# A one-core encoder layer: the stretch before the first products is rewritten, and phase 1 gets more load buffers

## The chip, the core and the metric

The kernel runs on one core of one Trainium2 chip. The metric is the device time of one execution in microseconds. Of three runs of the kernel before, the median is 971.41 us (969.67 to 974.25).

## The reference

The program computes one layer of an encoder over 512 rows of 2048 numbers (x), all in float32. What matters for the change is its front:

```
c_act = silu(c)                                   # c: 2048 numbers
mod   = c_act @ w_ada + b_ada                     # w_ada: 2048 x 6144
shift, scale, gate = split(mod, 3)
h     = rms_norm(x, norm_gain) * (1 + scale) + shift
proj  = h @ w_in                                  # w_in: 2048 x 7168
...                                               # attention on 8 heads, retention on 4 heads
x     = x + gate * (y @ w_out)                    # w_out: 2048 x 2048
return rms_norm(x, final_gain)
```

rms_norm divides each row by the root of the mean of its squares (plus 1e-6) and multiplies the columns by a gain.

## The kernel before

**Tiling.** The 512 rows are four row tiles t of 128; the 2048 columns are sixteen tiles k of 128. h is kept transposed, one tile of 128 x 512 for each k, split into a high part hh and a low part hl; each tile of w_in is split in the same way into whi and wlo by `conv` (ScalarE copies the high part, line 543, VectorE subtracts it, line 544). A product is three passes over TensorE (`mm3`, lines 85 and 87): high by high, high by low, low by high.

**The prelude** (lines 89 to 455) makes h of column tile k = 0 and x transposed (xT) for the other fifteen. Its loads all go through SyncE's queue, in this order: c, eight loads of w_ada (256 KB each: the columns of shift and of scale that belong to k = 0), the rows of b_ada and of the gain, then x in eight halves of 512 KB. ScalarE turns c into silu(c) (`ct`). VectorE multiplies the w_ada rows by `ct` and adds them up in `acc0` (lines 279 and 281), and four narrow products with a column of ones close the sum (`sums0`, line 288). For each row tile ScalarE takes the squares (line 302), VectorE and GpSimd make the root (lines 308, 315, 319), VectorE puts the factors on a diagonal (`dg`, line 327), TensorE turns x (line 343 by a transposition, line 351 by a product with the diagonal, which also scales), and the turned tile is scaled while it is read from PSUM (line 373). `pin` makes each engine keep to the written order of the pinned instructions.

**Phase 1** (lines 873 to 974) is thirteen units of 256 columns of w_in, taken through the sixteen k in chunks of 1, 2, 2, 3, 4 and 4 tiles. During one chunk the pieces that make the next chunk's modulation are spread between the fed items (`ada_pieces`): loads of w_ada into three buffers (AR = 3, lines 202 and 205), their weighted sums on VectorE (line 216), the closing sums (lines 230 and 244), then hh on ScalarE (line 168) and hl on VectorE (line 181). `feed` loads an item, splits it four items later (LEAD = 4) and multiplies it two items after that (LOOK = 2). The raw tiles of w_in have three buffers (RAW = 3). Sums of eleven units over the chunks are kept in SBUF and added to by VectorE (line 941; in the first chunk ScalarE copies them, line 939).

**Order.** Loads of w_in and w_ada share SyncE's queue, which works through its rows one after the other: a load whose buffer or whose semaphore is not free holds back all loads behind it. The program has eight semaphores for loads, given out in turn over both hardware queues (DMAHW0 to DMAHW7 in the rows below), so a load waits until the one that had the same semaphore has landed.

## Time and profile before

| | |
|---|---|
| span of the profiled execution, which is also its time in the profile | 971.6 us |
| TensorE busy in it | 941.5 us |
| VectorE busy in it | 618.0 us |
| first product of phase 1 begins | 28.75 us after the span's start |
| chunk 0 of phase 1 ends, first product of chunk 1 | 49.2 us, 53.18 us |

Positions are microseconds from the start of the span. The page's second part cuts the span into 40 slices of 24.3 us; the stretch that the change touches is slices 1 to 9. Where a row of a window gives busy time, a stretch minus the busy time is idle time, and PEclk below 1.00 is a TensorE clock below full speed.

### The profile page before, as it was taken

What the parts mean: (1) busy time and instruction counts of PE and PEld (TensorE: products, weight loads), DVE (VectorE), ACT (ScalarE), POOL (GpSimd) and SP (SyncE); (2) the same over time, 40 slices, a digit from 0 to 9 for tenths busy, and PEclk for the clock granted to TensorE, in tenths of its full rate; (3) what the DMA queues carried; (4) which work ended last, traced back from release to release, by engine and by line L of the source; (5) the groups of instructions that cost most, each with busy time, mean ns of one, the idle gap of its engine ahead of it and who ended that gap; (6) DMA issues with size and microseconds to landing.
All of it is one profiled execution on the core that took longest, in us unless ns stands there. A gap on an engine that the chain in (4) does not pass through costs nothing.

```text
span 971.6 us, 14377 instructions
## 1 busy us (share of the span) xinstructions
PE 941.5 (97%) x5556; PEld 820.4 (84%) x5556; DVE 618.0 (64%) x1101; ACT 376.5 (39%) x732; POOL 10.6 (1%) x22
## 2 busy tenths in 40 slices
PE   5989898999999999999999999999999999999996
PEld 4877687788988888988998899988899988888896
DVE  5879978977968786664555556745534382535444
ACT  3824242525235555444343232422333372333321
POOL 0000000000000000000000000000000000000001
PEclk9989999999999999999999999999999999999999
DMA  9786878763552222212224525425322148233304
GB/s 316 232 260 209 270 250 290 266 202 99 183 179 84 65 66 66 65 45 88 84 69 161 186 66 184 143 88 198 126 63 90 57 159 283 86 128 134 109 1 173
DMA packets 109715, 141.49 MB, mean 146 GB/s; under 512 B 6024, under 2 KB 78408, under 8 KB 109648
## 3 DMA queue, kind: packets, MB, share of 16 engines
q1 hardware_dynamic: 108496, 138.49, 43.4%
q10 hardware_dynamic: 1152, 2.10, 0.6%
q8 instruction: 43, 0.70, 0.3%
q14 instruction: 24, 0.20, 0.1%
HBM read 136.36 MB, written 4.20 MB: 145 GB/s over the span
## 4 chain that ended last, share of the span: by engine, by line
PE 89%; DMA 5%; DVE 3%; issue 2%; SPq 1%; ACT 0%; POOLq 0%; POOL 0%; DVEq 0%; ACTq 0%
PE pp L87 26%; PE pw L87 14%; PE pp L85 13%; PE po L87 12%; PE pw L85 7%; PE po L85 6%; PE op L87 3%; PE sp L87 2%; DMA raw<-in_w_in_dram 2%; DMA araw<-in_w_ada_dram 2%; PE op L85 2%; PE tp L770 1%; DVE aacc L216 1%; PE sp L85 1%; DMA xt<-in_x_dram 1%
## 5 line engine op out<-in xcount | busy, mean ns | idle before, releaser
L543 ACT CAST whi<-raw 128x512 fp32r<-128x512 f32 (+1 forms) x289 | 174.9, 606 | 435.8 <-PE pp L87 204.9
L544 DVE TENSOR_TENSOR wlo<-raw,whi 128x512 fp32r<-128x512 f32 (+1 forms) x289 | 193.9, 672 | 209.6 <-ACT whi L543 205.3
L85 PE MATMUL pp<-whi,hh 128*128 128x256 f32 x576 | 162.4, 282 | 0.0
L87 PE MATMUL pp<-wlo,hh 128*128 128x256 f32 x576 | 161.9, 281 | 0.0
L87 PE MATMUL pp<-whi,hl 128*128 128x256 f32 x576 | 161.5, 280 | 0.0
L85 PEld LDWEIGHTS pp<-whi,hh 128*128 128x128 f32 x576 | 108.5, 188 | 2.5 <-ACT sc L839 1.7
L87 PEld LDWEIGHTS pp<-wlo,hh 128*128 128x128 f32 x576 | 108.5, 188 | 1.0 <-DVE wlo L544 0.2
L87 PEld LDWEIGHTS pp<-whi,hl 128*128 128x128 f32 x576 | 108.5, 188 | 0.0
L85 PE MATMUL pw<-hh,whi 128*128 128x512 f32 x256 | 102.5, 401 | 3.6 <-DVE acc L941 3.6
L85 PE MATMUL pp<-hh,whi 128*128 128x512 f32 x256 | 102.7, 403 | 3.3 <-ACT hh L168 2.9
L87 PE MATMUL pp<-hh,wlo 128*128 128x512 f32 x256 | 102.1, 399 | 0.0
L87 PE MATMUL pp<-hl,whi 128*128 128x512 f32 x256 | 101.6, 397 | 0.0
L87 PE MATMUL pw<-hh,wlo 128*128 128x512 f32 x256 | 101.3, 396 | 0.0
L87 PE MATMUL pw<-hl,whi 128*128 128x512 f32 x256 | 101.1, 395 | 0.1
L87 PE MATMUL po<-wlo,yh 128*128 128x512 f32 (+1 forms) x252 | 92.6, 367 | 0.0
L85 PE MATMUL po<-whi,yh 128*128 128x512 f32 (+1 forms) x252 | 92.5, 367 | 0.0
L87 PE MATMUL po<-whi,yl 128*128 128x512 f32 (+1 forms) x252 | 92.5, 367 | 0.0
L216 DVE SCALAR_TENSOR_TENSOR aacc<-araw,ct,aacc 128x512 f32<-128x512 f32 (+2 forms) x75 | 76.1, 1014 | 10.8 <-DMA araw<-in_w_ada_dram 10.3
L941 DVE TENSOR_TENSOR acc<-acc,pw 128x512 f32<-128x512 f32 x100 | 66.3, 682 | 7.8 <-PE pw L87 7.3
L991 DVE SCALAR_TENSOR_TENSOR gacc<-graw,ct,gacc 128x512 f32<-128x512 f32 x60 | 45.0, 750 | 38.3 <-DMA graw<-in_w_ada_dram 38.0
L85 PEld LDWEIGHTS pp<-hh,whi 128*128 128x128 f32 x256 | 48.8, 191 | 16.7 <-ACT hh L168 3.0
L85 PEld LDWEIGHTS pw<-hh,whi 128*128 128x128 f32 x256 | 48.1, 188 | 17.3 <-DVE acc L941 5.7
(232 smaller groups left out, 1555.3 us busy)
## 6 DMA issues: line engine op xcount, KB each, us to landing
raw<-in_w_in_dram SPq DMA_DIRECT2D x94, 512.0 KB, 3.5
araw<-in_w_ada_dram SPq DMA_DIRECT2D x32, 512.0 KB, 5.5
graw<-in_w_ada_dram SPq DMA_DIRECT2D x64, 256.0 KB, 2.9
raw<-in_w_out_dram SPq DMA_DIRECT2D x32, 512.0 KB, 3.5
araw<-in_w_ada_dram SPq DMA_DIRECT2D x40, 256.0 KB, 3.7
raw<-in_w_in_dram SPq DMA_DIRECT2D x16, 384.0 KB, 5.4
araw<-in_w_ada_dram SPq DMA_DIRECT2D x16, 384.0 KB, 3.7
xt<-in_x_dram SPq DMA_DIRECT2D x8, 512.0 KB, 8.6
```

The source lines that it names most:

```text
L85: nc.tensor.matmul(o, lh, rh, start=start, stop=False, skip_group_check=True)
L87: nc.tensor.matmul(o, a, b, start=False, stop=stop and b is (rl if swap else rh), skip_group_check=True)
L216: ins = nc.vector.scalar_tensor_tensor(acc[:, :, :n], rv[:, a], ct[:, kr + a : kr + a + 1], acc[:, :, :n], op0=ALU.mult, op1=ALU.add,)
L543: c1 = nc.scalar.copy(dh, src)
L544: c2 = nc.vector.tensor_tensor(dl, src, f32(dh), op=ALU.subtract)
L770: nc.tensor.transpose(tp_[:, j * P : (j + 1) * P], pt[:, j * P : (j + 1) * P], ident)
L941: nc.vector.tensor_tensor(accs[u][i], accs[u][i], ps[i], op=ALU.add)
L991: nc.vector.scalar_tensor_tensor(st["acc"], raw, ct[:, kr : kr + 1], st["acc"], op0=ALU.mult, op1=ALU.add)
```

## The change

- **Loads of the prelude.** x goes through ScalarE's queue in four loads of 1 MB; w_ada's first columns go through SyncE's in four loads of 512 KB, behind c; the rows of b_ada and of the gain go through GpSimd's queue.
- **x is scaled first, then turned.** Once a row tile's factor is known, VectorE multiplies x itself by it (`scaled`, in three pieces of 128, 896 and 1024 columns), TensorE only transposes, and the result is copied out of PSUM by ScalarE (three banks) and VectorE (one bank). The diagonal, its spreading over the partitions and the products with it are gone. The squares of a tile are split: ScalarE takes 1024 columns, VectorE the other 1024; ScalarE takes those of the next tile before it copies out this one.
- **w_ada's first columns** are no longer summed by VectorE. TensorE multiplies them by `ct` directly: 32 products of a 128 x 128 tile with one column, sixteen ahead of the last row tile's first transposition and sixteen behind it.
- **Phase 1.** w_ada has six buffers (AR = 6) in place of three, and w_in in the first four chunks three more (`raw1`). In these chunks an item is split eight items after it is fed (LEAD1 = 8) in place of four. All loads of chunk 0 are issued ahead of its first item.

ScalarE, from the start of its program. `ce` is the first step of silu(c), `xt` a row tile of x, `sq` and `sqa` the squares. Before:

```order
L144 ACT_TABLE_LOAD
L144 ACTIVATE ce<-ps_145 128x16 [waits PE_49]
L302 ACTIVATE sq,ssx<-xt_122 128x1024 [waits DMAHW3_49]
L302 ACTIVATE sq,ssx<-xt_122 128x1024 [waits DMAHW4_49,Activation_49]
L302 ACTIVATE sq,ssx<-xt_125 128x1024 [waits DMAHW5_49,Activation_49]
```

After:

```order
L121 DMA xt_107<-in_x_dram 128x2048
L121 DMA xt_108<-in_x_dram 128x2048
L121 DMA xt_109<-in_x_dram 128x2048
L121 DMA xt_110<-in_x_dram 128x2048 [waits DMAHW3_49]
L145 ACT_TABLE_LOAD
L145 ACTIVATE ce<-ps_135 128x16 [waits PE_49]
L300 ACTIVATE sqa,ssx<-xt_107 128x1024 [waits DMAHW0_49]
```

Four loads now stand ahead of the table load and of `ce`, and the fourth waits for the semaphore DMAHW3, which it shares with an earlier load.

TensorE, the end of the prelude and the first products (`pw`). `raw_105` and `raw_106` are the first columns of w_ada, for shift and for scale; `xt_109` and `xt_110` are the last two row tiles. After:

```order
L328 MATMUL psx<-ident,xt_109 128x128 x7
L286 MATMUL psa<-ct,raw_105 128x1 [waits DMAHW2_49]
L286 MATMUL psa<-ct,raw_105 128x1 x7
L286 MATMUL psa<-ct,raw_106 128x1 [waits DMAHW3_49]
L286 MATMUL psa<-ct,raw_106 128x1 x7
L322 MATMUL psk_285<-ident,xt_110 128x128 [waits DMAHW3_49,DVE_49,PE_49]
L286 MATMUL psa<-ct,raw_105 128x1 [waits DMAHW5_49]
L286 MATMUL psa<-ct,raw_105 128x1 x7
L286 MATMUL psa<-ct,raw_106 128x1 [waits DMAHW6_49]
L286 MATMUL psa<-ct,raw_106 128x1 x7
L328 MATMUL psx<-ident,xt_110 128x128 [waits DVE_49,PE_49,Activation_49]
```

The first load of `raw_106` is the one whose semaphore the fourth load of x waits for. Before, the place of these products was four, early in the prelude:

```order
L343 MATMUL psx<-ident,xt_122 128x128 x3
L288 MATMUL psa<-ones,acc_160 128x1 [waits DVE_49]
L288 MATMUL psa<-ones,acc_160 128x1
L288 MATMUL psa<-ones,acc_161 128x1 [waits DVE_49]
L288 MATMUL psa<-ones,acc_161 128x1
L331 MATMUL psb<-dg,ones 128x128 [waits DVE_49]
```

VectorE, one row tile of the prelude after the change (`sqd` is the squares' waste, `ms` the mean, `rsx` the factor that GpSimd makes, `xT` x transposed):

```order
L305 ISA sqd,ssx<-xt_108 128x1024 [waits DMAHW4_49]
L305 ISA ssx 128x1
L308 SCALAR_TENSOR_TENSOR ms_202<-ssx 128x1 [waits DVE_49,Activation_49]
L336 COPY xT_93<-psx 128x2x128 [waits PE_49]
L336 COPY xT_94<-psx 128x128
L276 COPY bg<-ps_135 128x48 [waits PE_49]
L277 TENSOR_SCALAR bg<-bg 128x16 [waits DVE_49]
L316 TENSOR_SCALAR xt_108<-xt_108,rsx 128x128 [waits Pool_49]
L316 TENSOR_SCALAR xt_108<-xt_108,rsx 128x896
L316 TENSOR_SCALAR xt_108<-xt_108,rsx 128x1024
```

All of a tile's squares, its copies and its scaling stand in one row; the next tile's squares come behind them.

The diff, cut to its core:

```diff
@@ -37,15 +37,13 @@
 N_PERSIST = 2
 ADA_SPAN = 0.65
 TAB_SPAN = 16
-WARM = 9
-WARM2 = 1
-LATE_AT = 7, 8
+WARM = 10, 3, 3
 LAG = 3
-RAW, WB, LOOK, LEAD, EB, YB = 3, 3, 2, 4, 1, 22
+RAW, RAW1, WB, LOOK, LEAD, LEAD1, EB, YB = 3, 3, 3, 2, 4, 8, 1, 22
 GR = 2
 GATE_RATE = 0.9
 N_FIRST = 13
-AR = 3
+AR = 6
@@ -73,7 +71,13 @@
     def f32(ap):
         return ap.bitcast(F32)
+    early = {"on": True, "n": 0}
     def raw_tile():
+        early["n"] += 1
+        if early["on"] and early["n"] % 2 == 0:
+            return aap.tile([P, 1024], F32, tag="raw1", name="raw1", bufs=RAW1)
         return wp.tile([P, 1024], F32, tag="raw", name="raw", bufs=RAW)
...
+    raw0 = [xp.tile([P, NK, P], F32, name=f"raw0{b}") for b in range(2)]
+    xn = [xp.tile([P, D], F32, name=f"xt{t}") for t in range(NT)]
+    def load0(q, b, i):
+        q.dma_start(
+            raw0[b][:, i * 8 : (i + 1) * 8],
+            wa[i * 8 * P : (i + 1) * 8 * P, b * D : b * D + P].rearrange("(a p) f -> p a f", p=P),
+        )
+    for t in range(NT):
+        nc.scalar.dma_start(xn[t], x2[t * P : (t + 1) * P, :])
+    nc.sync.dma_start(c_row, c.rearrange("b (k p) -> (b k) p", p=P))
+    for i in range(2):
         for b in range(2):
-            nc.sync.dma_start(
-                rv[:, :, b],
-                wa[n * 4 * P : (n + 1) * 4 * P, b * D : b * D + P].rearrange("(a p) f -> p a f", p=P),
-            )
-            if n + b == 0:
-                nc.sync.dma_start(c_row, c.rearrange("b (k p) -> (b k) p", p=P))
-        raw0.append(rv)
-        if n == 1:
-            nc.sync.dma_start(bg_row[0:32, :], b_ada[:, 0 : 2 * D].rearrange("b (k p) -> (b k) p", p=P))
-            nc.sync.dma_start(bg_row[32:48, :], norm_gain.rearrange("b (k p) -> (b k) p", p=P))
+            load0(nc.sync, b, i)
+    nc.gpsimd.dma_start(bg_row[0:32, :], b_ada[:, 0 : 2 * D].rearrange("b (k p) -> (b k) p", p=P))
+    nc.gpsimd.dma_start(bg_row[32:48, :], norm_gain.rearrange("b (k p) -> (b k) p", p=P))
...
-    acc0 = [aap.tile([P, 2 * P], F32, tag="acc0", name="acc0") for _ in range(2)]
-    for k in range(NK):
-        rv, c1 = raw0[k // 4][:, k % 4], ct[:, k : k + 1]
-        if k < 2:
-            nc.vector.tensor_scalar_mul(acc0[k], rv, c1)
-        else:
-            nc.vector.scalar_tensor_tensor(acc0[k % 2], rv, c1, acc0[k % 2], op0=ALU.mult, op1=ALU.add)
-    rsb = aap.tile([P, S], F32, name="rsb", bufs=1)
...
+    def turn_rows():
+        pin(nc.tensor.transpose(ps0[:, 64:112], bg_row, ident[0:48, 0:48]))
+        pin(nc.vector.tensor_copy(bg, ps0[:, 64:112]))
+        pin(nc.vector.tensor_scalar_add(bg[:, 16:32], bg[:, 16:32], 1.0))
+    psa = bank(psA, "psa")
+    psk = bank(psA, "psk")
+    def sums0(b, i):
+        for a in range(8 * i, 8 * i + 8):
+            pin(
                 nc.tensor.matmul(
+                    psa[:, b : b + 1], raw0[b][:, a, :], ct[:, a : a + 1],
+                    start=a + b == 0, stop=a == NK - 1, skip_group_check=True,
                 )
+            )
+    def shift_scale0():
+        pin(nc.vector.tensor_tensor(sv[:, 0:1], psa[:, 0:1], bg[:, 0:1], op=ALU.add))
+        pin(nc.vector.tensor_tensor(av[:, 0:1], psa[:, 1:2], bg[:, NK : NK + 1], op=ALU.add))
+        pin(nc.vector.tensor_tensor(av[:, 0:1], av[:, 0:1], bg[:, 32:33], op=ALU.mult))
+    def squares_a(t):
+        sa = aap.tile([P, 1024], F32, tag="araw", name="sqa", bufs=AR)
+        marks["sq"] = pin(nc.scalar.activation(sa, xn[t][:, 0:1024], AF.Square, accum_out=ssx[:, t, 0:1]))
+    def squares(t):
+        sd = aap.tile([P, 1024], F32, tag="aacc", name="sqd")
+        v = xn[t][:, 1024:2048]
+        pin(nc.vector.tensor_tensor_reduce(sd, v, v, 1.0 / D, EPS, ALU.mult, ALU.add, ssx[:, t, 1:2]))
+        ms = small.tile([P, 1], F32, tag="ms1", name="ms1", bufs=2)
         pin(
             nc.vector.scalar_tensor_tensor(
+                ms, ssx[:, t, 0:1], 1.0 / D, ssx[:, t, 1:2], op0=ALU.mult, op1=ALU.add
             )
         )
+        nc.gpsimd.tensor_tensor(rsx[:, t : t + 1], ms, mhalf[:, 0:1], op=ALU.pow)
+    def scaled(t, a, b):
+        v = xn[t][:, a:b]
+        marks["sc"] = pin(nc.vector.tensor_scalar_mul(v, v, rsx[:, t : t + 1]))
     psx = {}
+    def k0_part(t):
+        o = psk3[:, 0:P] if t == 3 else psk[:, t * P : (t + 1) * P]
+        pin(nc.tensor.transpose(o, xn[t][:, 0:P], ident))
+    def turned(t, b, pin=pin):
         ps = psx[t, b] = bank(psP, "psx")
         for j in range(b == 0, 4):
             k = 4 * b + j
             pin(nc.tensor.transpose(ps[:, j * P : (j + 1) * P], xn[t][:, k * P : (k + 1) * P], ident))
+    def evacuated(t, b, eng):
         for i, g in enumerate(groups):
             lo, hi = max(g[0], 4 * b), min(g[-1] + 1, 4 * b + 4)
             if i and lo < hi:
+                dst = xt_tiles[i][:, lo - g[0] : hi - g[0], t * P : (t + 1) * P]
+                src = psx[t, b][:, (lo - 4 * b) * P : (hi - 4 * b) * P].rearrange("p (k f) -> p k f", k=hi - lo)
+                pin(eng(dst, src))
+    act, dve = nc.scalar.copy, nc.vector.tensor_copy
...
-    for _ in range(WARM):
-        pin(nc.tensor.matmul(ps0[:, 128:256], ones, ident, start=True, stop=True))
-    turned(0, 0)
-    turned(0, 1)
-    for _ in range(WARM2):
-        pin(nc.tensor.matmul(ps0[:, 128:256], ones, ident, start=True, stop=True))
-    turned(0, 3)
-    for t in range(2):
-        squares(t, 0)
-        squares(t, 1)
-    roots(0)
-    psa = sums0()
-    psk = bank(psA, "psk")
-    diagonal(0)
-    shift_scale0(psa)
-    spread(0)
-    k0_part(0)
-    spread_out(0)
-    for t in range(2):
-        turned_scaled(t, 2)
-        evacuated(t, 2)
-        squares(t + 2, 0)
-        squares(t + 2, 1)
-        scaled(t, 0)
-        turned(t + 1, 0)
-        half_root(t + 1)
...
+    def warm(n):
+        for _ in range(n):
+            pin(nc.tensor.matmul(ps0[:, 128:256], ones, ident, start=True, stop=True))
+    warm(WARM[0])
+    squares_a(0)
+    for t in range(NT):
+        squares(t)
+        if t:
+            evacuated(t - 1, 0, dve)
         if t == 1:
+            turn_rows()
+        if t == 3:
+            psk3 = bank(psM, "psk3")
+            sums0(0, 0)
+            sums0(1, 0)
+        scaled(t, 0, P)
+        k0_part(t)
+        if t == 3:
+            break
+        scaled(t, P, 1024)
+        turned(t, 0)
+        turned(t, 1)
+        scaled(t, 1024, D)
+        turned(t, 2)
+        turned(t, 3)
+        if t < 2:
+            warm(WARM[1 + t])
+        squares_a(t + 1)
+        for b in range(1, 4):
+            evacuated(t, b, act)
+    sums0(0, 1)
+    marks["conv1"] = [marks["sq"], marks["sc"]]
+    sums0(1, 1)
+    scaled(3, P, 1024)
+    shift_scale0()
     A, B = slice(0, 3 * P), slice(3 * P, S)
     h0_sum(A, psk[:, A])
     h0_sum(B, psk3[:, 0:P])
     h0_low(A)
     h0_low(B)
+    scaled(3, 1024, D)
+    for b in range(4):
+        turned(3, b, lambda ins: ins)
+    late = [lambda b=b: evacuated(3, b, act if b % 2 else dve) for b in range(4)]
...
             if item["load"]:
                 item["load"]()
             loaded.append(item)
-        if len(loaded) > (LEAD if item is not None else 0):
+        lead = LEAD1 if early["on"] else LEAD
+        while len(loaded) > (lead if item is not None else 0):
             it = loaded.pop(0)
             pending.append((it, it["conv"]()))
-        if len(pending) > (LOOK if item is not None else 0):
+            if item is None:
+                break
+        while len(pending) > (LOOK if item is not None else 0):
             flush_one()
+            if item is None:
+                break
...
-    for i, f in zip(LATE_AT, late):
-        agenda.setdefault(i, []).append(f)
+    for i, f in enumerate(late):
+        agenda.setdefault(LEAD1 + LOOK + i, []).append(f)
...
+        early["on"] = ci < len(CHUNKS) - 2
...
+        if ci == 0:
+            for it in items:
+                it["load"]()
```

More of the change, by code (lines that the diff above doesn't have):

```diff
@@ L282, in trunk_kernel @@
-    rsb = aap.tile([P, S], F32, name="rsb", bufs=1)
-    def sums0():
-        psa = bank(psA, "psa")
-        for i in range(2):
-            for b in range(2):
+    def turn_rows():
[7 more added lines that the diff above has]
+            pin(
@@ L288, in sums0 @@
                 nc.tensor.matmul(
-                    psa[:, b : b + 1], acc0[i][:, b * P : (b + 1) * P], ones[:, 0:1],
-                    start=i + b == 0, stop=i == 1, skip_group_check=True,
-                )
-        return psa
-    def shift_scale0(psa):
-        nc.vector.tensor_tensor(sv[:, 0:1], psa[:, 0:1], bg[:, 0:1], op=ALU.add)
-        nc.vector.tensor_tensor(av[:, 0:1], psa[:, 1:2], bg[:, NK : NK + 1], op=ALU.add)
-        nc.vector.tensor_tensor(av[:, 0:1], av[:, 0:1], bg[:, 32:33], op=ALU.mult)
@@ L299, in squares @@
-    def squares(t, h):
-        sq = xp.tile([P, 1024], F32, tag="sq", name="sq")
-        v = xn[t][:, h * 1024 : (h + 1) * 1024]
-        marks["sq"] = pin(nc.scalar.activation(sq, v, AF.Square, accum_out=ssx[:, t, h : h + 1]))
-    mss = {}
-    def half_root(t):
-        ms = mss[t] = small.tile([P, 2], F32, tag="ms2", name="ms2", bufs=2)
-        pin(nc.vector.tensor_scalar(ms[:, 0:1], ssx[:, t, 0:1], 1.0 / D, EPS, op0=ALU.mult, op1=ALU.add))
-    def roots(t):
-        if t not in mss:
-            half_root(t)
-        ms = mss[t]
+                    psa[:, b : b + 1], raw0[b][:, a, :], ct[:, a : a + 1],
@@ L314, in roots @@
+    def squares(t):
[3 more added lines that the diff above has]
+        ms = small.tile([P, 1], F32, tag="ms1", name="ms1", bufs=2)
         pin(
             nc.vector.scalar_tensor_tensor(
-                ms[:, 1:2], ssx[:, t, 1:2], 1.0 / D, ms[:, 0:1], op0=ALU.mult, op1=ALU.add
+                ms, ssx[:, t, 0:1], 1.0 / D, ssx[:, t, 1:2], op0=ALU.mult, op1=ALU.add
@@ L317, in roots @@
             )
         )
-        nc.gpsimd.tensor_tensor(rsx[:, t : t + 1], ms[:, 1:2], mhalf[:, 0:1], op=ALU.pow)
-    dgs = {}
-    psbs = {}
-    def diagonal(t):
-        dg = dgs[t] = xp.tile([P, P], F32, tag="dg", name="dg", bufs=2)
-        marks["dg"] = pin(nc.vector.tensor_scalar_mul(dg, ident, rsx[:, t : t + 1]))
-    def spread(t):
-        psb = bank(psA, "psb")[:, 0:P]
-        pin(nc.tensor.matmul(psb, ones, dgs[t], start=True, stop=True))
-        psbs[t] = psb
-    def spread_out(t):
-        pin(nc.vector.tensor_copy(rsb[:, t * P : (t + 1) * P], psbs[t]))
+        nc.gpsimd.tensor_tensor(rsx[:, t : t + 1], ms, mhalf[:, 0:1], op=ALU.pow)
@@ L343, in turned @@
             pin(nc.tensor.transpose(ps[:, j * P : (j + 1) * P], xn[t][:, k * P : (k + 1) * P], ident))
-    def turned_scaled(t, b):
-        ps = psx[t, b] = bank(psP, "psx")
-        for j in range(4):
-            k = 4 * b + j
-            pin(
-                nc.tensor.matmul(
-                    ps[:, j * P : (j + 1) * P], xn[t][:, k * P : (k + 1) * P], dgs[t], start=True, stop=True
-                )
-            )
-    def pieces(b):
+    def evacuated(t, b, eng):
         for i, g in enumerate(groups):
@@ L429, in trunk_kernel @@
-    marks["conv1"] = [marks["sq"]]
-    psk3 = bank(psM, "psk3")
-    turned_scaled(2, 2)
-    turned_scaled(2, 3)
-    roots(3)
-    scaled(2, 0)
-    turned(3, 0)
-    diagonal(3)
-    marks["conv1"].append(marks["dg"])
-    k0_part(3)
+    def warm(n):
[7 more added lines that the diff above has]
+            evacuated(t - 1, 0, dve)
+        if t == 1:
+            turn_rows()
[18 more added lines that the diff above has]
+            evacuated(t, b, act)
@@ L439, in trunk_kernel @@
+    sums0(0, 1)
[3 more added lines that the diff above has]
+    shift_scale0()
     A, B = slice(0, 3 * P), slice(3 * P, S)
-    evacuated(2, 2)
     h0_sum(A, psk[:, A])
-    scaled(2, 1)
-    turned(3, 1)
     h0_sum(B, psk3[:, 0:P])
@@ L446, in trunk_kernel @@
     h0_low(B)
-    spread(3)
-    turned(3, 2)
-    evacuated(2, 3)
-    turned(3, 3)
-    spread_out(3)
-    scaled(3, 0)
-    scaled(3, 1)
-    late = [lambda b=b: scaled(3, b) for b in (2, 3)]
+    scaled(3, 1024, D)
+    for b in range(4):
+        turned(3, b, lambda ins: ins)
+    late = [lambda b=b: evacuated(3, b, act if b % 2 else dve) for b in range(4)]
     x_scope.close()
```

41 lines of the change are left out of this document (removed).

## The prediction

> **What bounds the kernel now.** I read the page first.
>
> ```profile
> span 971.6 us, 14377 instructions
> PE 941.5 (97%) x5556; PEld 820.4 (84%) x5556; DVE 618.0 (64%) x1101; ACT 376.5 (39%) x732; POOL 10.6 (1%) x22
> PE   5989898999999999999999999999999999999996
> DVE  5879978977968786664555556745534382535444
> ```
>
> TensorE is busy for 941.5 of 971.6 us, so the change can win only what TensorE loses outside its work: about 30 us, and what it does at a lower clock. The second row of digits shows VectorE near its limit in the slices up to 200 us. Then I asked for windows, to see where TensorE's losses lie (columns: the stretch, its length, busy time of PE, PEld, DVE, ACT, POOL with counts, PEclk, share of the DMA engines, GB/s).
>
> ```profile
> 48.00:50.00 2.00, 1.60 (x12) 1.12 (x10) 1.73 (x3) 0.37 (x1) 0.00 (x0) 1.00 0.88 288
> 50.00:52.00 2.00, 0.23 (x3) 0.15 (x2) 0.39 (x3) 0.20 (x1) 0.00 (x0) 1.00 1.09 368
> 52.00:54.00 2.00, 0.82 (x2) 0.73 (x3) 1.56 (x3) 2.00 (x4) 0.00 (x0) 0.54 1.06 328
> 54.00:56.00 2.00, 2.00 (x8) 1.71 (x8) 1.90 (x4) 0.45 (x1) 0.00 (x0) 0.50 0.69 255
> 56.00:58.00 2.00, 2.00 (x6) 1.55 (x6) 1.62 (x3) 0.00 (x0) 0.00 (x0) 0.50 0.39 102
> 58.00:60.00 2.00, 2.00 (x8) 1.57 (x7) 0.00 (x0) 0.33 (x1) 0.00 (x0) 0.75 0.86 245
> 110.00:116.00 6.00, 4.60 (x20) 3.09 (x18) 5.83 (x9) 1.13 (x2) 0.00 (x0) 1.00 0.80 267
> 116.00:122.00 6.00, 4.46 (x31) 3.99 (x31) 4.46 (x7) 3.01 (x13) 0.00 (x0) 1.00 0.83 284
> 140.00:170.00 30.00, 26.27 (x162) 22.48 (x162) 25.46 (x35) 7.11 (x13) 0.00 (x0) 1.00 0.83 284
> ```
>
> TensorE idles 0.40 + 1.77 + 1.18 = 3.35 us at the border from chunk 0 to chunk 1, then works at a reduced clock (0.82 x 0.46 + 2 x 0.5 + 2 x 0.5 + 2 x 0.25 = 2.9 us lost); it idles 1.40 + 1.54 = 2.94 us at 110 to 122, and 30.00 - 26.27 = 3.73 us at 140 to 170. Together **12.9 us**. The rest lies ahead of the first product and at the kernel's end. The chain of waits says what ended these stalls:
>
> ```profile
> 44.91 6.79 DMA raw<-in_w_in_dram
> 51.80 0.62 ACT whi L543
> 52.41 0.72 ACT hh L168
> ...
> 113.54 5.24 DMA araw<-in_w_ada_dram
> ...
> 144.99 5.78 DMA araw<-in_w_ada_dram
> ```
>
> At 51.8 the high part of a w_in tile waited for a load issued at 44.9, and hh of chunk 1 stood behind it on ScalarE. The later ones are VectorE's sums, waiting for w_ada with three buffers.
>
> **The change part by part. (a) What the loads now wait for.** ScalarE's fourth load of x waits until the first load of `raw_106` has landed, and behind it stand the table load, silu(c), and so all of VectorE's prelude. I call the time of that landing R. Rows for the rates:
>
> ```profile
> 2.00:13.00 11.00, 4.17 (x20) 3.77 (x20) 5.84 (x19) 0.20 (x2) 0.00 (x0) 1.00 0.99 286
> 13.00:21.50 8.50, 6.58 (x40) 5.91 (x41) 4.75 (x19) 6.01 (x10) 1.11 (x2) 0.80 1.03 413
> 0.73 1.28 ACT L144 ACT_TABLE_LOAD   x1 [0.73 <-PEq L1296]
> 5.56 0.35 DVE L279 TENSOR_SCALAR acc<-araw,ct 128x256 f32<-128x256 f32 x1 [0.35 <-DMA araw<-in_w_ada_dram]
> ```
>
> The first stretch is w_ada alone (286 GB/s), the second x alone (413 GB/s). Two loads of w_ada (1.05 MB) cost 3.7 us, each load of x (1.05 MB) 2.5 us. Data flows from about 2.3 us, and I estimate 1.3 us from last byte to release, from VectorE's first sum: it waited until 5.56 for the first two loads, whose 0.53 MB at 286 GB/s from 2.3 us were through at 4.2. If both queues get equal bytes, R = 2.3 + 3.7 + 2.5 + 1.3 = 9.8. If the three loads of x go wholly first, R = 2.3 + 7.6 + 3.7 + 1.3 = 14.9. No row shows two queues with unequal rows at once. I take **R = 10.5**, nearer the even end since both queues start together, and keep both ends.
>
> **(b) From R to the first product.** The fourth load's issue 0.5, the table load 1.28, then silu to `ct` 0.9 (ScalarE 0.18 and three small VectorE steps): R + 2.7. Then VectorE's chain per row tile:
>
> ```profile
> L755 DVE CUSTOM_DVE_ANT_0 pt<-sp,ad 128x512 f32<-128x512 f32 x32 | 21.0, 685 | 0.5 <-PE sp L87 0.5
> L762 DVE TENSOR_SCALAR pt<-pt,den 128x512 f32<-128x512 f32 x32 | 15.5, 484 | 0.6
> L802 DVE TENSOR_SCALAR dt<-dlt,lg 128x896 f32<-128x896 f32 x4 | 2.7, 682 | 0.0
> L327 DVE TENSOR_SCALAR dg<-ident,rsx 128x128 f32<-128x128 f32 x4 | 1.1, 287 | 0.7 <-POOL rsx L319 0.4
> 16.61 0.56 POOL L319 TENSOR_TENSOR rsx<-ms,mhalf 128x1 f32<-128x1 f32 x1 [15.11 <-DVE ms L315]
> ```
>
> Squares of 1024 columns: 0.685 for 512, so about 1.3 with the read of the sum; the mean 0.16; the root 0.75 from mean to next VectorE step (16.45 to 17.20 before), filled by the copies of the last tile; scaling 0.29 + 0.68 + 0.75 (128, 896, 1024 columns, the last drawn out from 0.484 and 0.682). Sum 3.9, with gaps 4.0. Three tiles: 12.0, so R + 14.7. TensorE's last eight transpositions of tile 2: 1.0. Then the 32 narrow products. Before, four took 0.95 us:
>
> ```profile
> L281 DVE SCALAR_TENSOR_TENSOR acc<-araw,ct,acc 128x256 f32<-128x256 f32 x14 | 5.7, 478 | 0.0
> 15.56 0.95 PE L288 MATMUL psa<-ones,acc 128*128 128x1 f32 x8
> 18.14 1.92 PE L351 MATMUL psx<-dg,xt 128*128 128x128 f32 x8
> 22.43 1.06 PE L351 MATMUL psx<-dg,xt 128*128 128x128 f32 x8
> ```
>
> So 32 take **7.6 us**, where VectorE's sums (14 x 0.478 = 5.7 us, hidden under x's landing) and 0.95 us on TensorE stood. They are off VectorE, but pinned on TensorE behind tile 2, and nothing covers them: VectorE needs only 2.5 us for tile 3 up to its factor. 3.8 + 0.3 (tile 3's first transposition) + 3.8. Then shift and scale 0.45, with a low part of w_in (0.69) written between, and hh's first part 0.68: 1.8. First product: R + 14.7 + 1.0 + 7.9 + 1.8 = **R + 25.4 = 35.9**, against 28.75: a loss of **7.1 us**. The diagonal, its spreading and VectorE's scaled copies, all removed, are inside this count: the new chain replaces them.
>
> **(c) Chunk 0 to 1.** All w_in of chunk 0 and twelve of sixteen w_ada loads fit the new buffers and land while the prelude runs. So the load wait of 6.79 us disappears from the path. What is late next is VectorE:
>
> ```profile
> 28.75:49.20 20.45, 19.96 (x106) 16.10 (x105) 19.01 (x38) 16.32 (x32) 0.00 (x0) 1.00 0.72 222
> L216 DVE SCALAR_TENSOR_TENSOR aacc<-araw,ct,aacc 128x512 f32<-128x512 f32 x30 | 22.4, 747 | 1.0 <-DMA araw<-in_w_ada_dram 0.8
> L544 DVE TENSOR_TENSOR wlo<-raw,whi 128x512 fp32r<-128x512 f32 x271 | 186.3, 688 | 208.2 <-ACT whi L543 203.9 <-PE tp L770 2.6 <-PE sp L87 1.0
> L544 DVE TENSOR_TENSOR wlo<-raw,whi 128x256 fp32r<-128x256 f32 x18 | 7.6, 420 | 1.4 <-ACT whi L543 1.3
> ```
>
> Between the first hl and the second its list holds 18 sums (13.4), eight low parts (4.2), the last scaling and late copies (2.2), and shift, scale, h (2.9): 22.7 us, against 20.4 us that chunk 0's products took on TensorE (28.75 to 49.2). About 2 us of idling stays. That is shorter than the gap that brought the clock down before (50 to 53.2, with 0.23 us of work), so I add no loss of clock. The Trainium skill's page "TensorE: Matmul & The Clock Gate" (Part 1, What's actually happening) has the clock halved after an idle window of about 3.4 us; the trace agrees (PEclk 0.54 and 0.50 behind that gap).
>
> **(d) Later chunks.** With six w_ada buffers, loads are asked for twice as far ahead; from the second to the fourth h VectorE has slack over the products, so I count the gaps at 110 to 122 and 140 to 170 as gone. Bounds: nothing of them (6.7 us kept) to all. The later clearing of the queue at the change from eight items' lead to four moves program order only; its cost is at most one item's products, hidden by two split items in hand: nothing.
>
> **Sum.** 12.9 recovered, less 2.0 kept, less 7.1: 3.8 us. 971.6 - 3.8 = 967.8; the median of the runs shown is 0.2 below the profiled execution, so **967.6 us**.
>
> **Rivals.** *One: x starves w_ada.* R = 14.9; the rest as above: 967.6 + 4.4 = 972.0. For it: w_ada's rows are 512 bytes, x's 8 KB, so a queue served row by row gets a sixteenth; against it, no row shows it. The Trainium skill's page "DMA: Bandwidth & Descriptors" (Queues, rings and completion order) has each DMA engine take turns between queues by packets and not by bytes; that is this rival, and no run here shows it yet. The same page (Issuing engines are not separate DMA queues) says that issuing from several engines saves only issue time, which speaks against a gain from the second queue.
>
> *Two: nothing is kept.* R = 9.8 and VectorE keeps up at the first border: 967.6 - 0.7 - 2.0 = 964.9.
>
> ```profile
> 123.09 1.28 DVE L941 TENSOR_TENSOR acc<-acc,pw 128x512 f32<-128x512 f32 x2
> ```
>
> For it: neighbouring steps of VectorE overlap a little (two of this row take 1.28, 0.64 each, where a step of this size alone takes 0.69), which takes 22.7 down to about 21; against it, its waits for other engines in between.
>
>
> *Three: a cold TensorE.* Rows of the prelude before:
>
> ```profile
> 16.00:17.00 1.00, 0.51 (x5) 0.42 (x4) 0.38 (x3) 0.88 (x3) 0.39 (x1) 1.00 1.05 430
> 17.00:18.00 1.00, 0.46 (x4) 0.46 (x5) 0.36 (x2) 0.86 (x3) 0.16 (x1) 1.00 1.01 406
> 18.00:19.00 1.00, 1.00 (x8) 1.00 (x7) 0.90 (x5) 0.81 (x2) 0.00 (x0) 0.51 1.02 410
> ```
>
> Here TensorE was busy for half of 2 us, and the clock fell to 0.51. After the change it stands idle until R, and has 2.4 us of work per 4 us tile after it. If the clock is at half when the narrow products begin, they take 1.92 to 1.06 times as long: 7.6 becomes up to 13.8. At half rate for all: 967.6 + 6.2 = 973.8; together with the late R of rival one, which leaves it idle longer, 978.2. It decides where TensorE's share just before them is under about a half. For it: that fall; against it: 3.8 us of dense products should themselves raise the clock, so that the price falls on the first half at most.
>
> *Four: the stalls stay.* If VectorE's own work and not the loads made the gaps at 110 to 170, 6.7 us are not recovered: 974.3. For it: DVE 5.83 of 6.00 at 110 to 116; against it: its idle time behind w_ada loads there.
>
> **How the numbers follow.** A measurement of this kernel tells 0.5% (4.9 us) from no change, so faster means below 966.5 and slower above 976.3. The forecast has 0.42 (own range 964 to 971, two fifths of it faster); rival one 0.18 (same); rival two 0.25 (faster); rival three 0.10 (slower); rival four 0.05 (between). Faster 0.17 + 0.25 = 0.42, slower 0.10 and a little from four and one: 0.13, same 0.45. The range reaches from 962 (rival two with the chain of (b) a few us shorter) to 975 (rival three alone).
>
> **What would show it.** Right: ScalarE's table load begins at 10 to 12 us, the first product at 34 to 37, no load ends a stall of TensorE from 40 to 170, and TensorE is busy throughout 110 to 170. Rival one: a table load near 15 and a first product near 40. Rival three: PEclk at half in the 8 us before the first product. Rival four: gaps at 110 to 170 with VectorE full. The prediction is wrong if the first product comes before 31, since then (b) has a step that isn't on the path, or if chunk 1 begins later than 60.

## The result, and the profile after

The changed kernel takes 984.74 us (median of four runs, 982.26 to 986.62) beside 972.83 for the kernel before (969.67 to 976.39) on the same chip: a ratio of 1.013, with a 95% interval of 1.0095 to 1.0165. It is slower by 1.3%, and 17 us above the 967.6 that was predicted. Since the chips differ a little, times of different runs are compared below by their ratio to the kernel before, measured beside each.

The page of the changed kernel begins so (its profiled execution took 985.34 us):

```profile
span 983.5 us, 14417 instructions
PE 949.4 (97%) x5596; PEld 827.2 (84%) x5596; DVE 615.3 (63%) x1082; ACT 374.4 (38%) x735; POOL 11.8 (1%) x24
PE   2999999999999999999999999999999999999996
```

TensorE's share is the same 97%. What is new stands in the first digit: in the first 24.6 us it is now busy for two tenths. The timeline of ScalarE (start, length, instruction, and in brackets the idle time ahead of it and what ended it) says why:

```profile
0.74 14.43 ACTq L121 DMA_DIRECT2D xt<-in_x_dram  x4
15.19 1.28 ACT L145 ACT_TABLE_LOAD   x1 [15.19 <-DMA raw<-in_w_ada_dram]
```

The four loads of x took ScalarE's queue until 15.2 us, because the fourth waited for the first load of `raw_106` (w_ada's columns for scale). The table load, which stood at 0.73 before, follows at 15.19. The chain of waits has that load (start, length):

```profile
1.65 13.16 DMA raw<-in_w_ada_dram
```

So R, the time at which it has landed, was 14.8 and not 10.5. The DMA queues from 6 to 10 us (packets, MB, time of their packets as a share of 16 engines):

```profile
q10 hardware_dynamic: 200, 1.51, 92.0%
q1 hardware_dynamic: 202, 0.10, 8.9%
```

q10 carries x, q1 w_ada. Both moved the same number of packets, and x fifteen times as many bytes. (From 2 to 6 us, where the queues start up, it was 164 packets on q10 against 277 on q1.) This is the share that rival one gave to a queue that is served row by row. The rule of the Trainium skill that the prediction named for it ("DMA: Bandwidth & Descriptors", Queues, rings and completion order: turns by packets) is borne out by these two rows.

From there to the first product (TensorE's timeline; the last row is the first product):

```profile
30.72 3.63 PE L286 MATMUL psa<-ct,raw 128*128 128x1 f32 x32
34.21 0.40 PE L322 MATMUL psk<-ident,xt 128*128 128x128 f32 x1
34.40 6.83 PE L286 MATMUL psa<-ct,raw 128*128 128x1 f32 x32
43.27 0.79 PE L89 MATMUL pw<-hh,whi 128*128 128x512 f32 x1 [0.44 <-ACT hh L345]
```

(The profile counts two matmuls for each of the 32 narrow products, so x32 is half of them.) The first half of them took 3.63 us, the second 6.83. The windows show the clock (eighth column from the stretch: PEclk, ahead of the DMA share and GB/s):

```profile
32.00:34.00 2.00, 2.00 (x21) 2.00 (x20) 0.52 (x1) 0.00 (x0) 0.00 (x0) 1.00 0.72 227
34.00:36.00 2.00, 2.00 (x14) 2.00 (x13) 0.00 (x0) 0.00 (x0) 0.00 (x0) 0.57 0.01 1
36.00:38.00 2.00, 2.00 (x11) 2.00 (x11) 0.00 (x0) 0.00 (x0) 0.00 (x0) 0.50 0.00 0
42.00:44.00 2.00, 1.56 (x6) 1.06 (x6) 1.26 (x5) 1.80 (x4) 0.00 (x0) 0.50 0.00 0
44.00:46.00 2.00, 2.00 (x7) 1.52 (x6) 2.00 (x5) 0.64 (x2) 0.00 (x0) 0.50 0.00 0
46.00:48.00 2.00, 2.00 (x8) 1.60 (x7) 2.00 (x5) 0.00 (x0) 0.00 (x0) 0.51 0.40 112
48.00:50.00 2.00, 1.28 (x9) 0.95 (x8) 2.00 (x4) 1.27 (x3) 0.00 (x0) 1.00 0.77 246
```

TensorE counts as busy without a gap from 30.7 us, and yet the clock falls to half 3.6 us after the narrow products begin (at 34.3). It stays there until 48, so that chunk 0's first products run at half rate too: from 43.27 to 48 TensorE is busy for 4.73 us, and about half of that, 2.4 us, is lost. At 48 to 50 TensorE idles 0.72 us more: the next product waits until ScalarE has copied a bank out, which itself stood behind the last row tile's transpositions.

The stalls that the buffers were to remove, and one that is new (windows of the changed kernel):

```profile
100.00:130.00 30.00, 28.91 (x123) 21.73 (x121) 29.65 (x44) 12.84 (x29) 0.00 (x0) 1.00 0.87 296
130.00:170.00 40.00, 39.23 (x256) 35.63 (x257) 38.77 (x49) 9.80 (x18) 0.00 (x0) 1.00 0.87 295
290.00:300.00 10.00, 8.07 (x43) 6.67 (x42) 8.06 (x13) 2.92 (x5) 0.00 (x0) 0.86 0.65 210
600.00:700.00 100.00, 99.03 (x655) 89.34 (x655) 56.79 (x88) 31.18 (x57) 1.01 (x1) 1.00 0.48 153
64.00:66.00 2.00, 2.00 (x12) 1.64 (x11) 2.00 (x8) 1.67 (x3) 0.00 (x0) 1.00 1.07 364
```

From 100 to 170 TensorE loses 1.09 + 0.77 = 1.9 us instead of 6.7. The border to chunk 1 lies at 64 to 67 us here (the high part of its h begins at 64.9, its first product at 66.9); TensorE doesn't idle there (last row), and the clock stays up. But at 290 to 300, where it lost nothing before, it loses 1.93 us and about 1.1 us more at a reduced clock, and at 600 to 700 another 0.97. The same window before:

```profile
290.00:300.00 10.00, 10.00 (x49) 8.18 (x48) 9.18 (x20) 7.66 (x15) 0.00 (x0) 1.00 0.28 86
```

The waits of 250 to 300 us name the cause of the loss at 290 to 300 (us in total, times, longest; the first two rows after, the third before):

```profile
DVE gacc L942 <- DMA graw<-in_w_ada_dram: 9.1, 6, 2.2
PE pw L89 <- DVE acc L889: 1.9, 1, 1.9
DVE gacc L991 <- DMA graw<-in_w_ada_dram: 6.5, 6, 2.8
```

`graw` are the loads of w_ada for the gate, in two buffers. VectorE, in order, waits for them, and behind it stand the additions (`acc`) that empty TensorE's banks. Before, VectorE waited 6.5 us for these loads, and no bank was late. The first product came 14.5 us later than before (43.27 against 28.75), the last low part of h 7.9 us later (239.9 against 232.0), the end 11.9 us later.

### The profile page after: what moved, and what is told of

It reads as the page before. It is cut to its first block, busy times and chain, and to the rows that moved or that the text cites. A ratio compares the mean times of both kernels' runs of the same rounds, so it can differ in the third digit from the quotient of the medians.

```text
span 983.5 us, 14417 instructions
## 1 busy us (share of the span) xinstructions
PE 949.4 (97%) x5596; PEld 827.2 (84%) x5596; DVE 615.3 (63%) x1082; ACT 374.4 (38%) x735; POOL 11.8 (1%) x24
## 4 chain that ended last, share of the span: by engine, by line
PE 83%; DMA 7%; DVE 6%; issue 2%; ACT 1%; POOL 0%; SPq 0%; DVEq 0%; POOLq 0%; ACTq 0%
PE pp L91 22%; PE pw L91 13%; PE po L91 12%; PE pp L89 11%; PE pw L89 7%; PE po L89 6%; DMA graw<-in_w_ada_dram 4%; PE op L91 3%; PE sp L91 2%; PE op L89 2%; PE tp L717 1%; DMA raw<-in_w_ada_dram 1%; DVE wlo L486 1%; PE sp L89 1%; PE psa L286 1%
```

## The experiments

### One load of x moved

```diff
-    for t in range(NT):
+    for t in range(NT - 1):
         nc.scalar.dma_start(xn[t], x2[t * P : (t + 1) * P, :])
 ...
             load0(nc.sync, b, i)
+    nc.sync.dma_start(xn[NT - 1], x2[(NT - 1) * P : NT * P, :])
```

> The changed kernel with one load moved: the fourth 1 MB load of x is issued by SyncE behind the four loads of w_ada, so that ScalarE has only three loads ahead of its table load. Theory A (the late start comes from ScalarE, which stood at that fourth load until w_ada's first load had landed at 15 us, with the table load, silu and VectorE's squares behind it): the table load begins near 3 us, VectorE's first squares near 6, when the first row tile lands; the 13.4 us from the first squares to the narrow products then end near 20, the narrow products take 10.5 us more, and the first product comes at 31 to 34 instead of 43.3. The time falls by 8 to 11 us, to 974 to 977. Rival B (it is the sharing of the DMA engines itself: x's large rows hold w_ada back, and the narrow products wait for w_ada whatever ScalarE does): first product not before 38, time 980 or more.

Measured: ratio 1.0012 (0.9996 to 1.0027), 972.79 us; 1.2%, or 11.5 us, under the change. ScalarE's and TensorE's timelines:

```profile
2.28 1.28 ACT L146 ACT_TABLE_LOAD   x1 [2.28 <-issue]
18.42 3.91 PE L287 MATMUL psa<-ct,raw 128*128 128x1 f32 x32
23.65 6.83 PE L287 MATMUL psa<-ct,raw 128*128 128x1 f32 x32
32.52 0.80 PE L89 MATMUL pw<-hh,whi 128*128 128x512 f32 x1 [0.44 <-ACT hh L346]
```

Theory A holds in each of its steps (the first squares begin at 5.85), the time is a little under what it gave, and rival B falls. The late start, and with it nearly all of the loss, comes from one load that stood on ScalarE's queue ahead of other work. The clock falls here too, 3.2 us after the narrow products begin, at another time of the run (21.6 us; a window):

```profile
21.00:22.00 1.00, 1.00 (x10) 1.00 (x9) 1.00 (x1) 1.00 (x2) 0.00 (x0) 0.81 0.98 377
```

So it follows these products, and not a time of the run or the late start. That they are its cause is what the next two runs test.

### What brings the clock down

The first try put a 128-column product behind every second narrow one:

```diff
                     psa[:, b : b + 1], raw0[b][:, a, :], ct[:, a : a + 1],
                     start=a + b == 0, stop=a == NK - 1, skip_group_check=True,
                 )
             )
+            if a % 2:
+                pin(nc.tensor.matmul(psa[:, P : 2 * P], ones, ident, start=True, stop=True))
```

> The changed kernel with one 128-column product (ones times identity, its result unused) after every second narrow product, 32 in all over the four groups. Theory C (products of one column don't count as work for the clock: it halves some 3.5 us into them and stays halved into chunk 0): the clock stays at 1.00 from 34 to 48 us. The narrow products then take 64 x 0.113 = 7.2 us and the added ones 32 x 0.13 = 4.2, together 11.4 instead of 10.5, but chunk 0's first products run at full rate and gain about 2.5: the time falls by about 1.5 us, to 982 to 984. Rival D (the clock falls for another reason, such as the low share of work before, which a stretch of narrow products only follows): the clock still shows about 0.5 in 36 to 46, the added products cost 4 to 8 us, and the time is 988 or more.

Measured: ratio 1.0204 (1.0185 to 1.0223), 992.04 us. The added products open sums of their own (`start=True`) in the bank in which the sums of shift and scale still lie open. Most likely this kernel so leaves out part of shift and scale of column tile 0, which no run tests by itself; its time is that of all the products. Windows:

```profile
34.00:36.00 2.00, 2.00 (x16) 2.00 (x16) 0.00 (x0) 0.00 (x0) 0.00 (x0) 0.82 0.49 138
36.00:38.00 2.00, 2.00 (x11) 2.00 (x11) 0.00 (x0) 0.00 (x0) 0.00 (x0) 0.50 0.00 0
```

The clock fell all the same, at 35.3 instead of 34.3 us, and theory C fell in the form in which it was put; D was right on the time. But the later fall left another reading open: too few columns even so. The second try changes only the width of the narrow products:

```diff
-                    psa[:, b : b + 1], raw0[b][:, a, :], ct[:, a : a + 1],
+                    psa[:, b * P : (b + 1) * P], raw0[b][:, a, :], ct[:, a : a + 1].to_broadcast([P, P]),
```

> The changed kernel with the 64 narrow products widened: each multiplies by the same column of silu(c) laid out 128 times, so that it has 128 columns instead of one, with the same number of weight loads. Theory C2 (the clock follows the columns that stream through TensorE, and one-column products, alone or with one 128-column product to every two, stream too few of them; the run with wide products between fell 1 us later, and not never): each product takes 0.143 us as the transpositions of the same size do, the clock stays at 1.00 from 30 to 48 us, the 64 take 9.2 instead of 10.5 us, and chunk 0's first products gain about 2.5 us. The time falls by 3 to 4 us, to 981 to 982. Rival D2 (it is the f32 weight loads or something else of these products that brings the clock down): clock about 0.5 again from 34 us on, the 64 take about 16 us and the time is 990 or more.

Measured: ratio 1.0086 (1.0065 to 1.0107), 978.56 us; 0.44%, or 4.3 us, under the change. Timeline of TensorE, and a window:

```profile
31.27 3.74 PE L286 MATMUL psa<-ct,raw 128*128 128x128 f32 x32
34.95 3.74 PE L286 MATMUL psa<-ct,raw 128*128 128x128 f32 x32
40.26 0.50 PE L89 MATMUL pw<-hh,whi 128*128 128x512 f32 x1 [0.80 <-ACT hh L345]
34.00:38.00 4.00, 4.00 (x38) 4.00 (x38) 0.00 (x0) 0.00 (x0) 0.00 (x0) 1.00 0.25 69
```

The clock stays at 1.00, and all the products together take 7.5 us instead of 10.5: with 128 columns they cost no more than with one at full clock (3.74 against 3.63 us for the first half). The weight loads are the same, so D2 falls. That the one-column shape brings the clock down is shown; that the chip counts columns is the simplest reading of the two tries, and wasn't measured by itself.

### Each half of the change alone

Before's prelude with the changed phase 1 (AR 3 to 6, three further w_in buffers, a lead of eight, chunk 0's loads issued ahead):

```diff
-AR = 3
+AR = 6
+        if early["on"] and early["n"] % 2 == 0:
+            return aap.tile([P, 1024], F32, tag="raw1", name="raw1", bufs=RAW1)
 ...
+        if ci == 0:
+            for it in items:
+                it["load"]()
```

> The prelude of before (all loads on one queue, sums of w_ada on VectorE) with the change's phase 1: six w_ada buffers, three further w_in buffers, eight items' lead, chunk 0's loads issued ahead. The prediction's steps (c) and (d) put this part alone at 12.9 - 2.0 = 10.9 us: 962, with the first product at 28.7 as before. Rival E (the buffers are worth only the 5.5 to 6 us by which the changed kernel's delay shrank from 14.5 us at the first product to 8 to 9 at the end of phase 1): 967. Under F (part of the gain is given back later, where the gate's loads at 290 to 300 us stall TensorE): the phase's end comes 8 to 11 us earlier than before, the kernel's end only 6 to 8.

And the new prelude with phase 1 as before (AR 3, a lead of four, none of the further buffers, nothing issued ahead):

> The change's prelude with phase 1 as before: three w_ada buffers, three w_in buffers, four items' lead, nothing of chunk 0 issued ahead. If the two parts add up (the prelude costs 14.5 us at the first product and the half clock at chunk 0's start, the buffers give back about 6): 972.8 + 14.5 + 2 = 987 to 991. If the buffers bring nothing behind a late start, since the loads have had time to arrive anyhow: 983 to 986, the same as the changed kernel.

Measured: phase 1 alone 0.9999 (0.9981 to 1.0017), no gain at all; the prelude alone 1.0166 (1.0143 to 1.0188), 988.46 us, 3.5 us above the change, which the two intervals don't tell from nothing. In the phase-1-alone run the first product came at 30.9 instead of 28.75. Its border to chunk 1 still stalls (windows), and from 100 to 130 us 2.45 us stay:

```profile
52.00:54.00 2.00, 0.18 (x1) 0.19 (x2) 2.00 (x7) 1.05 (x2) 0.00 (x0) 1.00 1.09 354
56.00:58.00 2.00, 2.00 (x5) 1.57 (x6) 1.93 (x4) 0.00 (x0) 0.00 (x0) 0.50 1.02 324
```

The last low part of h came at 230.1, 1.9 us earlier than before: 4.1 us were recovered behind the first product. Theory F held in kind, though phase 1 came nowhere near 8 us ahead: what was ahead by then was lost again (a window, and the waits of 250 to 300 us):

```profile
280.00:290.00 10.00, 7.72 (x39) 6.31 (x39) 7.86 (x13) 2.76 (x5) 0.00 (x0) 0.86 0.67 210
DVE gacc L1005 <- DMA graw<-in_w_ada_dram: 10.0, 6, 2.7
PE pw L90 <- DVE acc L952: 2.3, 1, 2.3
```

This is the stall of the changed kernel at 290 to 300, without its prelude.

### One queue for everything

x's four loads on SyncE's queue behind those of w_ada:

```diff
-    for t in range(NT):
-        nc.scalar.dma_start(xn[t], x2[t * P : (t + 1) * P, :])
 ...
             load0(nc.sync, b, i)
+    for t in range(NT):
+        nc.sync.dma_start(xn[t], x2[t * P : (t + 1) * P, :])
```

> The changed kernel with x on SyncE's queue behind w_ada's four loads: one queue for all, in order. Theory A (ScalarE stood behind its fourth load, and w_ada was held back by x's large rows on the other queue): table load near 3 us, w_ada's 2 MB landed by 11 or 12 (they took until 15 and later), x's tiles 2.5 us apart from there, 13.6 to 21; chain of three tiles from 13.6 to 25.6, first product near 38 to 39; time 979 to 981. If x and w_ada are simply bound by the same DMA rate and nothing is gained by the order: first product at 43, time 984 to 985.

Measured: ratio 1.0127 (1.0109 to 1.0145). The first squares (VectorE's timeline) and the first product:

```profile
13.19 1.23 DVE L305 CUSTOM_DVE_ANT_0 sqd<-xt 128x1024 f32<-128x1024 f32 x1 [8.80 <-DMA xt<-in_x_dram]
40.82 0.80 PE L89 MATMUL pw<-hh,whi 128*128 128x512 f32 x1 [0.44 <-ACT hh L345]
```

Theory A was right on the mechanism (table load at 0.74, x's first tile at 13.2) and 2 us too early on the first product, since the first tile's fifteen transpositions took 3.46 us where the next tile's took 1.83. It gained 2.5 us at the first product and nothing measurable at the end: 3.0 us of TensorE's time are missing at 290 to 300 here (1.9 in the change), and 2.6 at 100 to 130 (1.1). With three tiles of x issued beside w_ada, and the fourth out of ScalarE's way, the first squares begin at 5.9; with w_ada first, at 13.2. So one queue in this order is worse than two. Whether one queue with x first would do as well as two was not run.

### The stall at 280 to 300 us

The first try to move it, with the gate's sums begun later:

```diff
-    gate = []
+    gate = [None] * 12
```

> The changed kernel with the gate's sums begun some 13 items (about 40 us) later: twelve empty steps stand ahead of them. Theory G (part of what phase 1 recovers is given back at 280 to 300 us, because VectorE, in order, waits 2.7 to 4.5 us at each of the gate's loads, with two buffers, just where the last chunk's sums out of TensorE's banks stand behind it): VectorE doesn't wait for these loads between 255 and 295, TensorE is busy throughout 280 to 300 (18.1 of 20 in the changed kernel, at a mean clock of 0.93) and the time falls by 2.5 to 4 us, to 981 to 982. Rival H (VectorE's own work and not the wait sets the pace there, or the loss moves to the place where the gate now stands): the time stays within 1 us of 984.7.

(In the change's trace the single waits are 0.7 to 2.2 us, 9.1 in all, and not 2.7 to 4.5 each.)

Measured: ratio 1.0176 (1.0156 to 1.0197), 0.5% worse than the change where a gain was expected. But the first of these sums began where it was (VectorE's timeline, of the changed kernel and then of this one):

```profile
257.56 0.47 DVE L940 TENSOR_SCALAR gacc<-graw,ct 128x512 f32<-128x512 f32 x1
```

```profile
257.19 0.48 DVE L940 TENSOR_SCALAR gacc<-graw,ct 128x512 f32<-128x512 f32 x1
```

Only the later sums moved (the last gate load from 691 to 734 us), and there TensorE lost 2.2 us at 500 to 600, where the change loses nothing; at 290 to 300 it idles 3.9 us instead of 1.9. The try says nothing on theory G. The same holds for the next run's second half, which had the same delay on top of before's prelude with the buffers, without chunk 0's loads ahead:

> The prelude of before with the change's six w_ada buffers, three further w_in buffers and eight items' lead, but without chunk 0's loads issued ahead, and with the gate's sums some 13 items later. If the loads ahead cost the 2.2 us by which the first product of the phase-1-alone run came later (30.9 against 28.75), and if theory G holds for the loss at 280 to 300, the first product comes at 28.7 and the time is 971.5 - 2.2 - 3 = 966 to 967. If neither holds: 971 to 973.

Measured: ratio 0.9989 (0.9972 to 1.0007). The first half of the expectation held: without the loads ahead the first product comes at 27.4 us instead of 30.9, so these loads cost 3.5 us of the start in that prelude. (That 27.4 is also 1.1 to 1.4 us earlier than in the two profiles of before's own program up to there, 28.75 and 28.48, stays open.) The last low part of h came at 224.4, 7.6 us earlier than before, and the end only 3.3 us earlier, since TensorE lost 2.9 us and some clock at 260 to 290.

What settles it is a third buffer for the gate's loads, made room for by letting the closing row share them:

```diff
-GR = 2
+GR = 3
 ...
-            row = pools["w"].tile([1, 512], F32, tag="grow", name="grow", bufs=1)
+            row = pools["w"].tile([P, 512], F32, tag="graw", name="grow", bufs=GR)[0:1, :]
```

In the changed kernel:

> The changed kernel with three buffers instead of two for the gate's loads (the row that closes a sum shares them, so that it fits). The run with the gate begun later left its first sixteen sums where they were, from 255 to 296 us, and so did not test theory G. Theory G (VectorE waits 9 us for these loads between 255 and 295, and TensorE's banks, to be emptied behind them, stall it for 1.9 us and bring its clock down): with a third buffer each load is issued one sum earlier, the waits fall to under 4 us, TensorE is busy throughout 280 to 300, and the time falls by 2.5 to 4 us against the changed kernel, to a ratio of 1.009 to 1.0105. Rival H (the waits have another cause, such as SyncE's queue, in which these loads stand behind loads of w_in that wait for VectorE): waits still 7 us or more, ratio 1.012 to 1.014.

in the kernel of the run above, without the delay:

> The prelude of before, the change's buffers and lead in phase 1 without chunk 0's loads ahead, and three gate buffers. The run like it with two gate buffers had its first product at 27.4 and its last low part of h at 224.4, 7.6 us earlier than before (232.0), but ended only 3.3 us earlier, since TensorE lost 2.9 us and some clock at 260 to 300. Theory G: that loss goes, and the time is 5 to 7 us under before, ratio 0.993 to 0.995. Rival H: the loss stays, ratio 0.996 to 0.999.

and in the kernel before:

> The kernel before with three gate buffers alone. Before, TensorE loses nothing at 260 to 300 us (20.00 of 20.00 twice), so theory G expects no gain here: ratio 0.998 to 1.002. If it is faster by more than 0.3%, what the third buffer brings in the other kernels isn't the loss that the change has made.

Measured: 1.0086 (1.0064 to 1.0108) instead of 1.013; 0.9929 (0.9905 to 0.9953) instead of 0.9989, where the delay went as well, so that this difference isn't the third buffer's alone; and 1.0011 (0.9994 to 1.0028) for the kernel before. Waits of 250 to 300 us and the window, for the changed kernel with the third buffer:

```profile
DVE gacc L942 <- DMA graw<-in_w_ada_dram: 2.6, 3, 1.1
290.00:300.00 10.00, 10.00 (x56) 8.56 (x56) 7.00 (x11) 5.29 (x10) 0.00 (x0) 1.00 0.33 106
```

Theory G holds in all three. In the changed kernel the wait falls from 9.1 to 2.6 us and the stall is gone; in the second kernel TensorE is busy throughout 260 to 300, where 2.9 us were missing; and the kernel before, which had no such stall, gains nothing although its waits fall in the same way (6.5 to 2.6 us). The third buffer is worth something only where phase 1 has been sped up.

### The change with three steps mended

The fourth load of x moved, the narrow products 128 columns wide, three gate buffers:

> The changed kernel with three of its steps mended: x's fourth load behind w_ada on SyncE's queue, the narrow products 128 columns wide, three gate buffers. The narrow products begin at 18.4 as in the run with the fourth load moved; at full clock they take 3.7 + 3.7 us, with the fourth tile's first transposition at 23.4 between them, so that the first product comes at 29 to 30 instead of 32.5, at full clock (2.5 us more). From that run's ratio of 1.001, less 2.5 to 3 us at the first product, 2 us of chunk 0's clock, and under theory G another 3: ratio 0.993 to 0.995; without theory G 0.996 to 0.998.

Measured: ratio 0.9928 (0.9908 to 0.9949), 964.33 us. TensorE's timeline:

```profile
18.60 3.74 PE L287 MATMUL psa<-ct,raw 128*128 128x128 f32 x32
23.42 3.74 PE L287 MATMUL psa<-ct,raw 128*128 128x128 f32 x32
28.72 0.50 PE L89 MATMUL pw<-hh,whi 128*128 128x512 f32 x1 [0.80 <-ACT hh L346]
```

Mended, the change is 0.7% faster than the kernel before, as fast as before's own prelude with the buffers (0.9929). Its first product comes at 28.72, before's at 28.75. So no run shows a gain from the new prelude, even mended. (The two kernels differ in the loads ahead too, which only the mended change has.) The gain is that of phase 1's buffers, once the gate's loads no longer give it back: 0.9929 with both, 1.0011 with the third gate buffer alone.

## Why the prediction was wrong, step by step

The sum of the prediction, beside what the profiles show (us against the kernel before):

| step | predicted | measured |
|---|---|---|
| first product | +7.1 | +14.5 |
| chunk 0's products at half clock | 0 | +2.4 |
| chunk 0's wait for a bank at 48 to 50, and smaller ones to 54 | 0 | +0.8 |
| border of chunk 0, stalls at 100 to 170 | -10.9 | -11.0 |
| stall at 290 to 300 | 0 | +3.1 |
| small losses at 240 to 260 and 600 to 700 | 0 | +1.4 |
| sum | -3.8 | +11.2 (spans: +11.9) |

**(a) R.** This step failed. It took 10.5, "nearer the even end since both queues start together". It was 14.8, next to the other bound (14.9). The mechanism, ScalarE standing at its fourth load, was right, and the first experiment shows that it is worth 11.5 us. Of the two bounds the wrong one was taken. The rows' sizes (8 KB against 512 bytes) were in hand and spoke for the late one; that both queues start together says nothing on the shares that they get. One row was misread as well: its 286 GB/s is not w_ada alone, since x's first rows fall into the last 4 us of the stretch. From 2 to 9 us, w_ada moves 1.90 MB, 271 GB/s. That shifts R by only 0.2 us.

**(b) From R to the first product.** The chain on VectorE was right: with R at 14.8, R + 15.7 puts the narrow products at 30.5 (30.72). That it comes out so close is in part luck, since it began a little early (17.29, where R + 2.7 gives 17.5) and took 13.4 us instead of 13.0. The narrow products were sized rightly at full clock (7.6; the wide ones took 7.5) and wrongly here (10.5). The argument against rival three, that "3.8 us of dense products should themselves raise the clock", failed too: products of one column bring it down, from 1.00 to 0.50 after 3.6 us. Rival three had the price (up to 6.2 us) and not the cause: the clock was at 1.00 when they began. The first product came 7.4 us later than forecast: 4.3 from R, 2.6 from the clock, 0.5 from the other steps. Nor did the sum reckon that the half clock lasts into chunk 0, which cost 2.4 us.

**(c) and (d) The buffers.** In the changed kernel they did in phase 1 about what was said. At the first border TensorE didn't idle at all, where 2.0 us were forecast, and the clock held; from 100 to 170 us 1.9 us stayed where nothing was. Rival four falls. But chunk 0 lasted some 3 us longer there (2.4 at half clock, 0.8 idle), and VectorE had that much more time, so the 2.0 of step (c) weren't tested. In the phase-1-alone run the border cost 1.98 us of idling, just the 2.0 of step (c), and then 1.7 us at a reduced clock (0.72 over the 5.9 busy us of 54 to 60), which (c) had ruled out: the 3.2 us of before aren't the shortest gap that brings the clock down. (In both runs 1.05 us of one-column products stand just ahead of the gap; whether they count towards it no run tests.) What no step had is the next late thing: VectorE's waits at the gate's loads. What is late next was asked at the first border only, and not behind phase 1, where work with two buffers of its own had been just in time. Phase 1 alone gave nothing instead of 10.9 us: 2.2 us went at the first product, which (c) had called covered, since the loads ahead "land while the prelude runs" (without them it came 3.5 us earlier); 5.7 us of the stalls were recovered instead of 10.9; and 3.8 us went at 280 to 300. Why the border doesn't stall without the loads ahead (6.00 of 6.00 at 48 to 54 in that run) stays open; there TensorE idles 1.8 us at 90 to 100 instead.

These sums rest on one profile each, and the stalls vary. The kernel before with a third gate buffer, whose program is the same up to the gate, loses 9.7 us at the border and from 100 to 170, where the profile of before loses 12.9. So a difference of some 3 us between two profiles of this stretch isn't shown, and the 5.7, -10.9 and -11.0 are no more exact than that.

**The rivals.** Rival one named what happened to R and had 0.18. The pair that the text put together, rival one with three (978.2), is the nearest case, 6.5 us short of 984.7. Its nearness is partly luck: it charged 6.2 us for the narrow products' clock, which cost 2.6, and nothing for chunk 0's half clock and the stall at 290 to 300. The range ended at 975, since the two rivals' prices were each weighed alone, though the text itself says that one makes the other likelier. Rival three was put down as slower, but its own price, 973.8, lies below the 976.3 that the text sets for slower; only the pair reaches it. The signs that the prediction named for rival one were met (a table load near 15, a first product beyond 40). Rival three's sign was met as well (PEclk at half in the 8 us before the first product), from another cause than the one it names. So was the prediction's own for being wrong: chunk 1 began at 64.9 (its h) and 66.9 (its first product), later than 60.

## What to carry to other kernels

A load on a compute engine's queue is an instruction of that engine. Before one is put there, count how many come ahead of the engine's first work and what each waits for, and when two queues run at once, reckon their shares by rows, not by bytes (here 200 and 202 packets in 4 us, of about 7.6 and 0.5 KB). Behind every stall that is removed, look for the next work with few buffers that was just in time, also far behind the place of the change: here two gate buffers took back what six w_ada buffers had won.
